# One PSUM bank for a scanned chunk, and a new order around it, in a hybrid decoder layer

## The chip, the cores and the metric

The kernel runs on one core of a Trainium2 chip. Its time is device time in microseconds (us) of one execution. TensorE (PE in the rows) multiplies, and its results go to PSUM, which holds eight banks of 128 partitions x 512 float32. VectorE (DVE) and ScalarE (ACT) read those banks; GpSimd (POOL) does small work and issues some transfers; SP issues the others. Each engine works through its own list of instructions in the order in which the program wrote them, and waits where an instruction needs something that is not there yet.

## The reference

One layer over 512 tokens of width 1024, all in float32:

```
u = rmsnorm(x); proj = u @ w_in            # retention q,k,v,gate; DeltaNet q,k,v,z,beta,a; two merge gates
ro = retention_chunkwise(rotary(rq), rotary(rk), rv)         # 8 heads, chunks of 128
y_ret = (silu(rgate) * groupnorm(ro)) @ w_ret_br
qkv = silu(causal_dwconv(dq, dk, dv))                        # 8 heads of 128
do = gated_delta_chunkwise(l2norm(q), l2norm(k), v, g, beta) # 4 chunks of 128 per head, in turn
    # per chunk: v_new = u_n - w_n S ; o = q_n S + a_n v_new ; S = S d_n + k_n^T v_new
y_dn = (rmsnorm(do) * silu(dz)) @ w_dn_br
h = x + (sigmoid(gate_r)*y_ret + sigmoid(gate_d)*y_dn) @ w_o
h = h + conv_ffn(rmsnorm(h)); out = rmsnorm(h)
```

## The kernel before

Dense products are split into a high and a low part (`whi`, `wlo`), three matmuls for each block of 128 rows; such three are called a triple here. The names in the rows tell the stage: `pk`, `pq`, `pv` are the projections of a DeltaNet head's k, q and v, `pr` those of retention, `pz` the gates, `py` the branch and merge products. Then follow the output product (`po`) and the FFN (`pa`, `pb`, `pd`).

The DeltaNet heads come in two groups of four. `k_front`, `q_front` and `v_front` take a head's projections: a convolution of three DVE instructions on the PSUM bank, a silu on ACT, transposes on TensorE (`pkt`, `pqt`, `pvt`), norms, and for k the products `pkk`, from which DVE makes `A`. A head's decay tile `gb` is loaded from DRAM by `decay_tile` and passed twice through ACT (`Abs`, then `Exp`); `A` and the masked scores need it. `solve` and `solve_up` (`pm`) invert the triangular systems of a group, and then `scan` runs twice, for two pairs of heads side by side: for each of four chunks it multiplies the state by k (`psc<-Sn,k`), lets DVE make `R`, multiplies by the inverse (`psc<-R,tt`), lets ACT copy the result to `vn`, makes the state's update and the chunk's output from `vn`, and lets DVE make the next state `Sn`. `scan_end` normalises, and its transposes are `pot`.

Retention has four pairs of heads. `ret_back` starts one pair after the other: `ret_scores` (`prs`, `pkv`), `ret_state` (`rS`, a chain of DVE and ACT), `ret_out` (`pro`, 28 row entries of the trace on two banks), and `ret_norm`, in which DVE reads both `pro` banks twice before they are free (`st`, then `ro`); its transposes are `proT`.

All PSUM tiles come from one pool of eight banks (`PS(name)`). A new tile takes a free one, and its first product waits until the last reader of the tile that held the bank before is done. The order of work is not written by hand. While the program is being built, a planner (`Order`) keeps a clock that each product advances by an assumed time (`Products.turn` and `Products.matmul`), and an assumed end for each DVE, ACT and POOL instruction. Side tasks (generators) are put between the dense products when that clock reaches their time. So the numbers of the planner set only the order in the lists. The lists themselves are fixed when the kernel runs.

Of the kernel before, what the change touches and what calls it, by code (L numbers as in the profile page):

```python
# [13 lines left out]
AF = mybir.ActivationFunctionType  # L14
ALU = mybir.AluOpType
# [4 lines left out]
P = 128  # L20
T = 512
D = 1024
NT = T // P
# [181 lines left out]
class Products:  # L205
# [3 lines left out]
    part = other = False  # L209

    def turn(self, part, other):


        if part != self.part:
            self.order.product(0.1)
        if self.other and not other:
            self.order.product(0.08)
        self.part, self.other = part, other

    def matmul(self, out, lhsT, rhs, start, stop, **kw):  # L220
        m = max(lhsT.shape[-1], out.shape[-1])
        if lhsT.dtype == F32R:
            self.turn(False, False)
            self.order.product(0.0135 + max(256, out.shape[-1]) / 2400)
        else:
            self.turn(min(lhsT.shape[0], lhsT.shape[-1]) < P, True)
            self.order.product(0.0107 + max(2 * m, 4 * out.shape[-1], 64) / 2400)
        self.engine.matmul(out, lhsT, rhs, start=start, stop=stop, **kw)  # L228

    def transpose(self, out, in_, identity):  # L230
# [5 lines left out]
def body(nc, tc, ctx, io):  # L236
# [3 lines left out]
    vec = Engine(order, "vec", nc.vector, vec_cost)  # L240
    act = Engine(order, "act", nc.scalar, act_cost)
    pool = Engine(order, "pool", nc.gpsimd, pool_cost)
    pe = Products(order, nc.tensor)
# [22 lines left out]
    def PS(name):  # L266
        return psp.tile([P, T], F32, name=name, tag="ps")

    def v3(ap, n=4):
        return ap.rearrange("p (n f) -> p n f", n=n)  # L270
# [384 lines left out]
    beta, G, nG, eG, egl, ekd = (hn(n) for n in ("beta", "G", "nG", "eG", "egl", "ekd"))  # L655
# [76 lines left out]
    def decay_tiles(hs):  # L732
        while "G" not in have:
            yield 0.3
        for h in hs:
            while h == GH and "up" not in heads[GH - 1]["got"] or h > GH and "o" not in heads[h - GH - 1]["got"]:
                yield 0.3
            spawn(decay_tile(h))
            yield 9.0 if h < GH else 4.0
# [11 lines left out]
    def conv_silu(ps, ci, name):  # L751
        w = prm[:, P_CW + 4 * ci:P_CW + 4 * ci + 4]
        acc = S(name)
        act.activation(acc, ps, AF.Identity, scale=w[:, 3:4])
        yield
        for j in (2, 1, 0):
            s = 3 - j
            vec.scalar_tensor_tensor(acc[:, s:], ps[:, :T - s], w[:, j:j + 1], acc[:, s:], ALU.mult, ALU.add)
        yield
        act.activation(acc, acc, AF.Silu)  # L760
        yield
        return acc

    GH = 4
# [20 lines left out]
    def k_front(hd, ps):  # L785
        h = hd["h"]
        kT = hd["kT"] = yield from conv_silu(ps, 8 + h, f"k{h}")
        yield PW
        pkt = transpose4(kT, "pkt")
        pkk = PS("pkk")  # L790
        for n in range(NT):
            pe.matmul(pkk[:, ck(n)], kT[:, ck(n)], kT[:, ck(n)], start=True, stop=True)
        yield -0.8
        A = hd["A"] = S(f"A{h}")
        ktok = hd["ktok"] = S(f"ktok{h}")
        ssk = s4("ssk")
        for n in range(NT):
            act.activation(A[:, ck(n)], pkt[:, ck(n)], AF.Square, accum_out=ssk[:, n:n + 1])
        while "G" not in have:
            yield 0.3  # L800
        for n in range(NT):
            act.activation(ktok[:, ck(n)], pkt[:, ck(n)], AF.Identity, scale=ekd[:, h, n:n + 1])
        yield -0.9
        vec.tensor_scalar(ssk, ssk, EPS, None, ALU.add)
        rk = s4("rk")
        yield
        rsqrt(rk, ssk)
        yield
        while h not in em:
            yield 0.3  # L810
        c1, c2, s = (mini.tile([P, 4], F32, name=n, tag=n, bufs=10) for n in ("c1", "c2", "sr"))
        vec.tensor_tensor(c1, beta[:, h], rk, ALU.mult)
        vec.tensor_tensor(s, c1, rk, ALU.mult)
        vec.scalar_tensor_tensor(c2, s, -1.0, eG[:, h], ALU.mult, ALU.mult)
        for n in range(NT):
            vec.scalar_tensor_tensor(A[:, ck(n)], pkk[:, ck(n)], s[:, n:n + 1], em[h][:, ck(n)], ALU.mult, ALU.mult)
        yield
        pool.affine_select(v3(em[h]), v3(em[h]), [[0, NT], [1, P]], ALU.is_ge, 0.0, base=0, channel_multiplier=-1)
        hd["c1"], hd["c2"] = c1, c2
        yield  # L820
        for b in range(4):
            sp.dma_start(a_dram[h // GH][b, h % GH].rearrange("n i j -> i n j"), v3(A)[R32[b], :, R32[b]])
        hd["got"].add("k")
# [130 lines left out]
    def scan(pair, i):  # L954

        while not all({"q", "v"} <= hd["got"] for hd in pair):
            yield 0.3
        E = range(len(pair))

        o = [hd["vtok"] for hd in pair]  # L960
        ssqo = [s4("ssqo") for _ in E]
        st = [None for _ in E]
        for n in range(NT):
            c = ck(n)
            ps = [v3(PS("psc")) for _ in E]
            R = [hd["vtok"][:, c] for hd in pair]
            if n > 0:
                for e in E:
                    pe.matmul(ps[e][:, 0], pair[e]["kT"][:, c], st[e], start=True, stop=True)
                yield  # L970
                R = [small.tile([P, P], F32, name="R", tag="R", bufs=4) for _ in E]
                for e, hd in enumerate(pair):
                    vec.scalar_tensor_tensor(R[e], ps[e][:, 0], hd["c2"][:, n:n + 1], hd["vtok"][:, c], ALU.mult, ALU.add)
                yield
            for e in E:
                pe.matmul(ps[e][:, 1], tt_all[:, (i + e) * NT + n], R[e], start=True, stop=True)
            yield
            vn = [small.tile([P, P], F32, name="vn", tag="vn", bufs=4) for _ in E]
            for e in E:
                act.copy(vn[e], ps[e][:, 1])  # L980
            yield
            for e, hd in enumerate(pair):
                if n < NT - 1:
                    pe.matmul(ps[e][:, 3], hd["ktok"][:, c], vn[e], start=True, stop=True)
                if n > 0:
                    pe.matmul(ps[e][:, 2], hd["qT"][:, c], st[e], start=True, stop=False)
                pe.matmul(ps[e][:, 2], hd["attn"][:, c], vn[e], start=(n == 0), stop=True)
            yield
            if n < NT - 1:
                for e, hd in enumerate(pair):  # L990
                    sn = small.tile([P, P], F32, name="Sn", tag="Sn", bufs=8)
                    if n == 0:
                        vec.tensor_copy(sn, ps[e][:, 3])
                    else:
                        vec.scalar_tensor_tensor(sn, st[e], egl[:, hd["h"], n:n + 1], ps[e][:, 3], ALU.mult, ALU.add)
                    st[e] = sn
                yield
            for e, hd in enumerate(pair):
                act.activation(o[e][:, c], ps[e][:, 2], AF.Identity, scale=hd["rqs"][:, n:n + 1])
                spawn(scan_ssq(o[e][:, c], ssqo[e][:, n:n + 1]), 0.4)  # L1000
            yield
        for e, hd in enumerate(pair):
            spawn(scan_end(hd, o[e], ssqo[e]), 0.8 + 0.8 * e)
# [75 lines left out]
    def ret_scores(hp):  # L1079

        pss = [PS("prs") for _ in range(2)]
        for n in range(NT):
            for r, ps in zip(E64, pss):
                pe.matmul(ps[:, ck(n)], rkT[n][r, hp], rqT[n][r, hp], start=True, stop=True)
        pk = PS("pkv")
        for n in range(NT - 1):
            for e, r in enumerate(E64):
                vv = rv[n][hp // 2][:, ck(2 * hp % 4 + e)]
                pe.matmul(pk[r, ck(n)], krot[n][:, hp, r], vv, start=True, stop=True)
        yield  # L1090
        states[hp] = [None]
        sTs = [S("sT") for _ in range(2)]
        for sT, ps in zip(sTs, pss):
            vec.tensor_tensor(v3(sT), v3(ps), umask.unsqueeze(1).to_broadcast([P, NT, P]), ALU.mult)
        return sTs, pk
# [58 lines left out]
    def ret_back():  # L1154
        while any(a is None for a in (*rqT, *rkT, *(b for a in rv for b in a))):
            yield 0.3
        for hp in range(4):
            while "up" not in heads[GH - 1]["got"]:
                yield 0.3
            sTs, pk = yield from ret_scores(hp)  # L1160
            yield from ret_state(hp, pk)
            spawn(ret_out(hp, sTs))
            yield 8.0
# [528 lines left out]
```

## Time and profile before

| | |
|---|---|
| three runs | 1001.25 us median (1001.21 to 1002.59) |
| the profiled execution | 1003.4 us, its span 1001.7 us |
| TensorE busy | 979.1 us, 98% of the span |
| VectorE / ScalarE / GpSimd busy | 72% / 53% / 17% |
| mean granted TensorE clock | 0.992 |

TensorE is busy in nearly every slice of the span. Its granted clock is a share of 2.4 GHz: 1.00 is that level, 0.50 is 1.2 GHz, and a stretch with a value between holds some of both. A busy engine at the lower level still counts as busy.

### The profile page before, as it was taken

Reading aid. Unit: us, or ns where it says so; the run is one execution under the profiler, and the core shown is the slowest. Engines: PE = TensorE matmul, PEld = TensorE weight load, DVE = VectorE, ACT = ScalarE, POOL = GpSimd, SP = SyncE. Lnnn points to the kernel's source line nnn. Section 1 sums busy time; section 2 is a strip of 40 time slices with the busy share of each in tenths; the row PEclk is TensorE's granted clock in tenths of the full one; section 3 lists DMA queues with packets and bytes.
Section 4 is the critical chain, followed back from the end, with each engine's and each line's share of the span. In section 5 each row is a group of like instructions: output and inputs, shape, how many; then the busy total and the mean of one; then the engine's idle time right before and its main releaser. Section 6 shows DMA issues by size and latency. Waiting matters only on the chain.

```text
span 1001.7 us, 14270 instructions
## 1 busy us (share of the span) xinstructions
PE 979.1 (98%) x5241; PEld 823.1 (82%) x5241; DVE 725.0 (72%) x1328; ACT 534.0 (53%) x1118; POOL 169.2 (17%) x214
## 2 busy tenths in 40 slices
PE   8999999998999999999999999899999999999997
PEld 7888888877888888888888878798888888888886
DVE  5777798565586797557699989965555667678785
ACT  5599312254865432476677565764443433356663
POOL 3021213222342310032000000121122221000001
PEclk9999999999899999999999999999999999999999
DMA  7243669886497694359986764566669999346663
GB/s 265 71 155 102 186 198 251 239 164 155 145 221 220 210 215 127 127 133 260 279 233 202 275 192 134 169 232 219 214 197 198 225 205 207 103 125 200 190 197 118
DMA packets 82230, 189.29 MB, mean 189 GB/s; under 512 B 22704, under 2 KB 31216, under 8 KB 82160
## 3 DMA queue, kind: packets, MB, share of 16 engines
q1 hardware_dynamic: 54640, 123.36, 38.1%
q0 software_dynamic: 27520, 65.02, 29.4%
q8 instruction: 41, 0.67, 0.3%
q14 instruction: 29, 0.24, 0.1%
HBM read 185.17 MB, written 68.19 MB: 253 GB/s over the span
## 4 chain that ended last, share of the span: by engine, by line
PE 88%; DVE 4%; ACT 3%; DMA 2%; issue 1%; POOL 1%; SPq 0%; POOLq 0%; ACTq 0%; DVEq 0%
PE py L228 14%; PE pb L228 12%; PE pa L228 12%; PE pd L228 10%; PE pr L228 9%; PE pz L228 9%; PE pv L228 4%; PE pq L228 4%; PE pk L228 4%; PE psc L228 3%; PE po L228 1%; PE pm L228 1%; DVE wlo L200 1%; PE pro L228 1%; DMA wraw<-s 1%
## 5 line engine op out<-in xcount | busy, mean ns | idle before, releaser
L200 ACT CAST whi<-wraw 128x1024 fp32r<-128x1024 f32 x212 | 219.3, 1035 | 157.2 <-PE pr L228 66.3
L200 DVE TENSOR_TENSOR wlo<-wraw,whi 128x1024 fp32r<-128x1024 f32 x212 | 254.8, 1203 | 62.5 <-ACT whi L200 59.3
L200 POOL TENSOR_SCALAR tock<-tick 128x1 f32<-128x1 f32 x72 | 33.7, 469 | 399.0 <-ACT tick L200 398.9
L200 DVE SCALAR_TENSOR_TENSOR acc<-pb,prm,acc 128x511 f32<-128x511 f32 (+1 forms) x44 | 33.0, 750 | 57.0 <-ACT acc L200 56.2
L228 PE MATMUL pa<-u2lo,whi 128*128 128x512 f32 (+1 forms) x192 | 71.4, 372 | 0.0
L228 PE MATMUL pa<-u2hi,whi 128*128 128x512 f32 (+1 forms) x192 | 71.4, 372 | 0.0
L228 PE MATMUL pa<-u2hi,wlo 128*128 128x512 f32 (+1 forms) x192 | 71.3, 371 | 0.0
L228 PE MATMUL pb<-u2hi,whi 128*128 128x512 f32 (+1 forms) x184 | 70.0, 380 | 0.0
L228 PE MATMUL pb<-u2lo,whi 128*128 128x512 f32 (+1 forms) x184 | 69.9, 380 | 0.0
L228 PE MATMUL pb<-u2hi,wlo 128*128 128x512 f32 (+1 forms) x184 | 69.9, 380 | 0.0
L228 PE MATMUL py<-whi,oh 128*128 128x512 f32 x160 | 62.7, 392 | 0.0
L228 PE MATMUL py<-wlo,oh 128*128 128x512 f32 x160 | 62.3, 390 | 0.0
L228 PE MATMUL py<-whi,ol 128*128 128x512 f32 x160 | 62.3, 389 | 0.0
L228 PE MATMUL pd<-whi,T 128*128 128x512 f32 (+1 forms) x198 | 55.3, 366 | 0.0
L228 PE MATMUL pz<-uhi,whi 128*128 128x512 f32 x128 | 51.8, 405 | 0.0
L228 PE MATMUL pr<-whi,uhi 128*128 128x512 f32 x128 | 51.2, 400 | 0.0
L228 PE MATMUL pr<-whi,ulo 128*128 128x512 f32 x128 | 50.0, 390 | 0.0
L228 PE MATMUL pz<-uhi,wlo 128*128 128x512 f32 x128 | 49.9, 390 | 0.0
L228 PE MATMUL pz<-ulo,whi 128*128 128x512 f32 x128 | 49.9, 390 | 0.0
L228 PE MATMUL pr<-wlo,uhi 128*128 128x512 f32 x128 | 49.9, 390 | 0.0
L200 DVE SCALAR_TENSOR_TENSOR acc<-pa,prm,acc 128x511 f32<-128x511 f32 (+1 forms) x44 | 33.0, 749 | 19.0 <-ACT acc L200 18.2
L200 ACT ACTIVATE acc<-pb,prm 128x512 f32<-128x512 f32 x22 | 17.2, 780 | 48.5 <-PE pb L228 48.5
(319 smaller groups left out, 2451.9 us busy)
## 6 DMA issues: line engine op xcount, KB each, us to landing
wraw<-w SPq DMA_DIRECT2D x100, 512.0 KB, 4.8
s<-wm POOLq DMA_DIRECT2D x30, 1024.0 KB, 8.8
wraw<-s SPq DMA_DIRECT2D x60, 512.0 KB, 3.9
s<-wd POOLq DMA_DIRECT2D x24, 704.0 KB, 5.5
wraw<-wm SPq DMA_DIRECT2D x30, 512.0 KB, 4.4
s<-s POOLq DMA_DIRECT2D x10, 1024.0 KB, 12.1
wraw<-wd SPq DMA_DIRECT2D x15, 512.0 KB, 3.7
s<-s POOLq DMA_DIRECT2D x8, 704.0 KB, 9.2
```

The source lines that it names most:

```text
L200: return f(out, *args, **kw)
L228: self.engine.matmul(out, lhsT, rhs, start=start, stop=stop, **kw)
```

## The change

It has four parts. In `scan`, a pair's chunk takes one PSUM bank in place of two: head e uses two quarters of it, `qa` for the product with the state and then for the output, `qb` for the product with the inverse and then for the state's update. In `ret_back`, a retention pair waits in the planner until both heads of the pair before are normalised, and 1.5 us more. In `decay_tiles` and `k_front`, a head of the second group (h >= 4) waits in the planner until head h-4 has left its scan (`"o"`): its decay tile, and now also its `pkt` and `pkk`. Last, the planner's clock for products on a part of the array is other: a turn costs 0.2 in place of 0.1, and such a product half of what it did, unless it is 64x64.

```diff
         if part != self.part:
-            self.order.product(0.1)
+            self.order.product(0.2)
...
-            self.turn(min(lhsT.shape[0], lhsT.shape[-1]) < P, True)
-            self.order.product(0.0107 + max(2 * m, 4 * out.shape[-1], 64) / 2400)
+            part = min(lhsT.shape[0], lhsT.shape[-1]) < P
+            self.turn(part, True)
+
+            two = part and tuple(lhsT.shape) != (64, 64)
+            self.order.product((0.0107 + max(2 * m, 4 * out.shape[-1], 64) / 2400) / (1 + two))
...
-            while h == GH and "up" not in heads[GH - 1]["got"] or h > GH and "o" not in heads[h - GH - 1]["got"]:
+            while h >= GH and "o" not in heads[h - GH]["got"]:
                 yield 0.3
             spawn(decay_tile(h))
...
         kT = hd["kT"] = yield from conv_silu(ps, 8 + h, f"k{h}")
+
+        while h >= GH and "o" not in heads[h - GH]["got"]:
+            yield 0.3
         yield PW
         pkt = transpose4(kT, "pkt")
...
-            ps = [v3(PS("psc")) for _ in E]
+
+
+            ps = v3(PS("psc"))
+            qa, qb = [ps[:, 2 * e] for e in E], [ps[:, 2 * e + 1] for e in E]
...
-                    pe.matmul(ps[e][:, 0], pair[e]["kT"][:, c], st[e], start=True, stop=True)
+                    pe.matmul(qa[e], pair[e]["kT"][:, c], st[e], start=True, stop=True)
...
-                pe.matmul(ps[e][:, 1], tt_all[:, (i + e) * NT + n], R[e], start=True, stop=True)
+                pe.matmul(qb[e], tt_all[:, (i + e) * NT + n], R[e], start=True, stop=True)
...
-                    pe.matmul(ps[e][:, 3], hd["ktok"][:, c], vn[e], start=True, stop=True)
+                    pe.matmul(qb[e], hd["ktok"][:, c], vn[e], start=True, stop=True)
                 if n > 0:
-                    pe.matmul(ps[e][:, 2], hd["qT"][:, c], st[e], start=True, stop=False)
-                pe.matmul(ps[e][:, 2], hd["attn"][:, c], vn[e], start=(n == 0), stop=True)
+                    pe.matmul(qa[e], hd["qT"][:, c], st[e], start=True, stop=False)
+                pe.matmul(qa[e], hd["attn"][:, c], vn[e], start=(n == 0), stop=True)
...
         for hp in range(4):
-            while "up" not in heads[GH - 1]["got"]:
+
+            while "up" not in heads[GH - 1]["got"] or len(normed) < 2 * hp:
                 yield 0.3
+            yield 1.5
             sTs, pk = yield from ret_scores(hp)
```

What this does to the lists is seen at three places. The first is TensorE's list at the second retention pair, during the first group's scans. Before, with the tiles' numbers:

```order
L228 MATMUL prs_2360<-rqT0_1465,rkT0_1674 128x128
L228 MATMUL prs_2361<-rqT0_1465,rkT0_1674 128x128
...
L228 MATMUL pkv_2370<-rv20_1845,krot2_1638 64x128 x2
L228 MATMUL psc_2395<-Sn_2325,k0_529 128x128
L228 MATMUL psc_2396<-Sn_2327,k1_643 128x128
L233 MATMUL proT_2403<-cst_101,ro_2351 128x128 x4
L228 MATMUL pq_2337<-uhi1_155,whi_1933 128x512
```

And now, from the same retention pair on:

```order
L236 MATMUL proT_2412<-cst_101,ro_2357 128x128 x4
L231 MATMUL prs_2417<-rqT0_1465,rkT0_1674 128x128
L231 MATMUL prs_2418<-rqT0_1465,rkT0_1674 128x128
...
L231 MATMUL pkv_2427<-rv20_1845,krot2_1638 64x128 x2
L231 MATMUL pq_2349<-uhi4_158,whi_1933 128x512
...
L231 MATMUL psc_2387<-R_2402,tt_178 128x128
L231 MATMUL psc_2387<-R_2403,tt_178 128x128
L236 MATMUL proT_2457<-cst_101,ro_2382 128x128 x4
L231 MATMUL psc_2468<-Sn_2435,k0_529 128x128
L231 MATMUL psc_2468<-Sn_2437,k1_643 128x128
```

The pair's scores now stand behind the first transposes of the pair before, dense triples follow them, and a chunk of two heads has one tile (`psc_2468`) where it had two (`psc_2395`, `psc_2396`). In the program as built, `psc_2396` took the bank of the second `pro` tile before it.

The second place is TensorE's list at the end of those scans, up to the k projection of head 5. Before (the third retention pair, in the middle of four chunks):

```order
L228 MATMUL pv_2624<-uhi2_156,whi_2007 128x512
...
L228 MATMUL prs_2649<-rqT0_1465,rkT0_1674 128x128
L228 MATMUL prs_2650<-rqT0_1465,rkT0_1674 128x128
...
L228 MATMUL pkv_2659<-rv01_2057,krot0_1605 64x128 x2
...
L228 MATMUL psc_2569<-R_2609,tt_178 128x128
L228 MATMUL psc_2570<-R_2610,tt_178 128x128
L228 MATMUL psc_2579<-R_2616,tt_178 128x128
L228 MATMUL psc_2580<-R_2617,tt_178 128x128
```

And now (the third pair comes when the scans are over, and `pkt`, `pkk` of head 4 come after it):

```order
L236 MATMUL proT_2666<-cst_101,ro_2627 128x128 x4
L231 MATMUL prs_2673<-rqT0_1465,rkT0_1674 128x128
...
L236 MATMUL pkt_2695<-cst_101,k4_2353 128x128 x4
L231 MATMUL pkk_2700<-k4_2353 128x128 x4
L236 MATMUL proT_2706<-cst_101,ro_2644 128x128 x4
L236 MATMUL pot_2721<-cst_101,vtok0_867 128x128 x4
L236 MATMUL pot_2731<-cst_101,vtok1_1002 128x128 x4
L231 MATMUL pv_2515<-uhi7_161,whi_2007 128x512
...
L231 MATMUL pk_2785<-uhi0_154,whi_2109 128x512
```

Head 4's k front has moved from the middle of the scans (behind `pq` of head 4) to their end, and the last product here, `pk_2785`, takes the bank of `pkt_2695`.

The third place is ScalarE's list there, now:

```order
L200 ACTIVATE roT2_2719<-proT_2666,prm_103 128x512
L200 ACTIVATE gb4_2671<-gb4_2671,nG_172 128x128 x4
L200 ACT_TABLE_LOAD
L200 ACTIVATE gb4_2671<-gb4_2671 128x512
L200 ACTIVATE A4_2751,ssk_2753<-pkt_2695 128x128 x4
L200 ACTIVATE ktok4_2752<-pkt_2695,ekd_175 128x128 x4
L200 ACTIVATE rS_2744<-rS_2744,cst2_102 128x128
L200 ACTIVATE roT3_2765<-proT_2706,prm_103 128x512
L200 ACTIVATE doT0_2767<-pot_2721,prm_103 128x512
...
L200 ACTIVATE gb6_2798<-gb6_2798,nG_172 128x128 x4
```

Before, the first tile of the four (`gb4`) stood far ahead, between the first chunk's copies:

```order
L200 COPY vn_2183<-psc_2148 128x128
L200 ACTIVATE gb4_2152<-gb4_2152,nG_172 128x128 x4
L200 ACT_TABLE_LOAD
L200 ACTIVATE gb4_2152<-gb4_2152 128x512
L200 COPY vn_2201<-psc_2178 128x128
```

The work on `gb4` has moved behind the scans, ahead of the two readers of `pkt_2695`, and on SP's list the loads of `gb6` and `gb7` now stand behind the four small transfers of head 4's `A`.

## Rows read from the trace of the kernel before

**Rows 1.** The page's head and its TensorE line.

```profile
span 1001.7 us, 14270 instructions
...
PE 979.1 (98%) x5241; PEld 823.1 (82%) x5241; DVE 725.0 (72%) x1328; ACT 534.0 (53%) x1118; POOL 169.2 (17%) x214
```

**Rows 2.** Stages: length, PE, PEld, DVE, ACT, POOL busy, PEclk, DMA share, GB/s.

```profile
220.00:225.00 5.00, 2.51 (x23) 1.83 (x23) 4.96 (x12) 1.74 (x2) 1.05 (x1) 0.99 0.67 106
225.00:230.00 5.00, 5.00 (x25) 4.18 (x24) 0.67 (x3) 3.38 (x17) 0.00 (x0) 0.67 0.86 212
...
245.00:250.00 5.00, 1.99 (x20) 1.64 (x22) 4.96 (x12) 0.63 (x1) 1.20 (x1) 0.88 0.64 76
250.00:255.00 5.00, 5.00 (x30) 4.67 (x27) 1.05 (x3) 2.00 (x12) 0.00 (x0) 0.50 1.08 270
255.00:260.00 5.00, 5.00 (x35) 4.61 (x35) 1.70 (x9) 4.66 (x19) 2.46 (x4) 0.94 0.37 129
```

**Rows 3.** All waits of TensorE from 195 to 285 us: total, times, longest.

```profile
PE psc L228 <- DVE ro L200: 1.9, 1, 1.9
PE prs L228 <- DVE q L200: 1.6, 1, 1.6
PE pkv L228 <- DVE ro L200: 1.3, 1, 1.3
PE pvt L233 <- ACT v L200: 1.0, 1, 1.0
PE prs L228 <- DVE ro L200: 0.7, 1, 0.7
PE psc L228 <- ACT ktok L200: 0.7, 1, 0.7
PE proT L233 <- DVE sT L200: 0.6, 1, 0.6
```

**Rows 4.** The chain that ended last, in order of time: start, us, what.

```profile
202.21 0.44 PE psc L228 x4
202.66 1.09 PE prs L228 x16
203.75 0.81 PE pkv L228 x12
...
208.82 1.38 PE pk L228 x6
...
211.09 3.10 PE pro L228 x28
...
221.97 1.27 DVE ro L200 x4
...
228.52 1.15 ACT A L200 x8
229.66 1.04 ACT ktok L200 x4
...
261.88 0.45 PE pot L233 x4
...
263.04 1.16 ACT gb L200 x4
264.22 1.28 ACT L200
265.52 0.63 ACT gb L200
```

**Rows 5.** TensorE in order of time, dense products after a scan product, and head 5's.

```profile
205.84 0.48 PE L228 MATMUL pk<-uhi,whi 128*128 128x512 f32 x1
206.16 0.39 PE L228 MATMUL pk<-ulo,whi 128*128 128x512 f32 x1
...
266.58 0.48 PE L228 MATMUL pk<-uhi,whi 128*128 128x512 f32 x1
```

**Rows 6.** Transfers of the decay tiles, 190 to 300 us.

```profile
DMA to landing us min/median/max: 3.1/8.2/9.9
```

More of the change, by code (lines that the diff above doesn't have):

```diff
@@ L972, in scan @@
                 for e, hd in enumerate(pair):
-                    vec.scalar_tensor_tensor(R[e], ps[e][:, 0], hd["c2"][:, n:n + 1], hd["vtok"][:, c], ALU.mult, ALU.add)
+                    vec.scalar_tensor_tensor(R[e], qa[e], hd["c2"][:, n:n + 1], hd["vtok"][:, c], ALU.mult, ALU.add)
                 yield
             for e in E:
-                pe.matmul(ps[e][:, 1], tt_all[:, (i + e) * NT + n], R[e], start=True, stop=True)
+                pe.matmul(qb[e], tt_all[:, (i + e) * NT + n], R[e], start=True, stop=True)
             yield
@@ L979, in scan @@
             for e in E:
-                act.copy(vn[e], ps[e][:, 1])
+                act.copy(vn[e], qb[e])
             yield
@@ L992, in scan @@
                     if n == 0:
-                        vec.tensor_copy(sn, ps[e][:, 3])
+                        vec.tensor_copy(sn, qb[e])
                     else:
-                        vec.scalar_tensor_tensor(sn, st[e], egl[:, hd["h"], n:n + 1], ps[e][:, 3], ALU.mult, ALU.add)
+                        vec.scalar_tensor_tensor(sn, st[e], egl[:, hd["h"], n:n + 1], qb[e], ALU.mult, ALU.add)
                     st[e] = sn
@@ L998, in scan @@
             for e, hd in enumerate(pair):
-                act.activation(o[e][:, c], ps[e][:, 2], AF.Identity, scale=hd["rqs"][:, n:n + 1])
+                act.activation(o[e][:, c], qa[e], AF.Identity, scale=hd["rqs"][:, n:n + 1])
                 spawn(scan_ssq(o[e][:, c], ssqo[e][:, n:n + 1]), 0.4)
```

## The prediction

> **What bounds the kernel now.** I read the page first: TensorE is busy 979.1 of 1001.7 us [rows 1]. So a reordering can win only what TensorE does not do at full speed: about 22 us of idle time, and the time in which it is busy at a lower clock, which the busy sum hides. The stages show where both lie. Nearly all of what this change touches is between 220 and 260 us, in the first group's scans: in 220 to 225 and in 245 to 250 TensorE is busy 2.51 and 1.99 of 5 us while VectorE is busy 4.96 of 5, and behind each of the two the granted clock is low, 0.67 in 225 to 230 and 0.50 (1.2 GHz) in 250 to 255 [rows 2]. The table of waits names the reason [rows 3]: in six waits, together 6.8 us, TensorE stands in front of a bank that a reader has not left: four on VectorE's `ro`, `q` and `sT` for the next retention pair, one on `ro` for a scan's product (1.9 us), one on ScalarE's `ktok`. The seventh, 1.0 us at about 274 us, waits for data (head 4's v behind the decay tiles on ScalarE). The chain of waits shows the same from the other side: VectorE's second `ro` runs from 221.97 to 223.24 [rows 4], as its list puts k's convolution and a weight's low part ahead of it, and TensorE's next product needs the bank that it reads.
>
> **How much is there.** I count the work of TensorE's list from the first scan product (202.21 us [rows 4]) to the first product of head 5's k (266.58 us [rows 5]), 64.4 us. Prices: a dense product 0.23 (1.38 for six), a scan product 0.22 (0.44 for two; the rows count each twice), a pair's scores 1.09 + 0.81, its outputs 3.10, four transposes 0.45 [rows 4], and 0.09 more for the first dense product after other work (0.32 between the two starts in place of 0.23 [rows 4, 5]). In the list: 63 dense (14.5), 68 scan products (15.0), three scores (5.7), three outputs (9.3), ten groups of transposes (4.5), `pkk` and `pqk` with eight products (1.8), nine returns to dense (0.8): 51.6 us. So 12.8 us of the 64.4 are lost. The six waits are 6.8 of them. The clock is another 4.7: (1 - 0.67) x 5 = 1.65, 0.50 x 5 = 2.5, 0.06 x 5 = 0.3, 0.05 in 220 to 225, and of the 0.6 in 245 to 250, in which TensorE mostly stood, some 0.2 [rows 2]. 1.3 us stay unnamed (hand-overs of a tenth or two each); I let them stay.
>
> **Part by part.** The *planner's clock* and its turns are numbers at build time; they cost nothing on the chip, and act only through the order. *One bank for a pair's chunk* takes four tiles out of each round of the two scans down to two, so that of eight banks two more are free for `prs`, `pkv`, `pro`. *Pairs in turn* moves each pair's `prs`/`pkv` behind the `proT` of the pair before, and so behind both of its `ro`. *Head 4's front held back* takes `pkt`/`pkk`, four `A` instructions and ScalarE's A and `ktok` (1.15 + 1.04 [rows 4]) out of the scans and puts them behind, with the tile's two passes and its table load (1.16 + 1.28 + 0.63 = 3.1 us [rows 4]), which stood at 202 us before.
>
> I then went through the changed lists of the three engines by hand from 202.2 us, each instruction at its duration before, and looked at each place where TensorE takes a bank or data:
> - The first retention pair ends on TensorE at about 216. VectorE's second `ro` still comes behind k's convolution and the weight's low part, and ends at about 225.8. The bank goes to `psc_2468`, which by the count of products ahead of it is issued at 228.7. The 1.9 us wait is gone, with 3 us to spare.
> - `psc_2387`'s R, then `Sn`, `vn`: VectorE and ScalarE are done 0.7 to 1.6 us ahead of TensorE each time, since three or four triples lie where none did.
> - The third pair's scores are issued at 244.2; their banks were left at 236 to 238. `pkk_2700` comes at 246.6, and the `ro` whose bank it takes ends at 242.9.
>
> So all six old waits have cover, and with them goes the cause of the low clock: 6.8 + 4.7 = 11.5 us. What hides the bank's readers is the dense triples of pq and pv that now stand between the scan's steps; without them the old waits come back. The 1.0 us wait for head 4's v also goes (ScalarE has its silu ready some 1.5 us ahead by the same count): 12.5.
>
> What is late next: by work alone TensorE comes to `pk_2785` at 202.2 + 47.3 = 249.5 (two outputs in place of three, nine groups of transposes, no `pqk`, eleven returns). It takes the bank of `pkt_2695`. ScalarE reads the last scan outputs until 245.4, `roT` until 246.0, then `gb4` 3.1, A 1.15, `ktok` 1.04: 251.3. A new wait of 1.3 to 1.8 us; I take 1.5. It is shorter than the pairs of waits that stood ahead of a low clock before, so I take no clock loss with it. Queued behind `ktok` on ScalarE are `roT3` and `doT0` to `doT3`, whose banks TensorE wants next; they follow within 2 us and TensorE has five triples by then. One more of the kind: head 5's q goes through ScalarE late, its transposes wait some 1.2 us at 271. The list has six more returns to dense over both groups: 6 x 0.09 = 0.5. In the second group I found no wait that the change touches; the scan is now spread over more gate triples and into the first `py`, so nothing is gained or lost there. The second solve keeps its place in TensorE's list within two triples.
>
> Sum: 12.5 - 1.5 - 1.2 - 0.5 = 9.3 us. The profiled execution took 1003.4 (span 1001.7 [rows 1] and 1.7 around it), 2.15 above the median of 1001.25; taken off the median the sum gives **992.0 us**, off the profiled one 994.1.
>
> **What the shared bank costs.** In the rows before, head 0's `Sn` may start when head 0's three products are done, as head 1's go to another bank. With one bank it starts after all six: 3 x 0.22 = 0.66 us later, and the steps at `R` and `vn` each wait for the second head's product, 0.22 each: 1.1 us for a chunk on the scan's own chain [rows 4]. I take it at nothing, since other triples cover it. The Trainium skill, "PSUM — Partial Sum Buffer", section "PSUM bank collisions raise a hardware error", asks for exactly this: two engines are to be kept apart by bank, not by address, even where one head's columns are not the other's. By that rule the sharing is not free; no run here shows it yet. If no triple covered it, three chunks of two groups would give 2 x 3 x 1.1 = 6.6 us.
>
> **The rivals.** *A, the forecast*: 992, range 989 to 994.5. The lower end is 12.5 with neither new wait at full size.
> *B, ScalarE becomes the late engine at `pk_2785`*: `gb4`'s load is issued behind a weight's load, by my count at 237; loads of these tiles took 3.1, 8.2 at the middle and 9.9 us at most [rows 6]. At 9.9 it lands at 247 and `ktok` at 252.3; a later issue adds as much. With some 3 us of wait there and the clock low for 4 to 5 us after it (2 to 2.5 more), the time is 992 + 4 = 996. For it: ScalarE's list has no gap there. Against it: at 8.2 the tile is there first.
> *C, the shared bank's chain shows*: 992 + 6.6 = 998.6, or the old waits return at other banks. Against it: the margins above are 0.7 us and more at nearly every step.
> *D, slower*: `gb6` and `gb7` stand on SP behind head 4's `A`, which stands behind `gb4`. If each load takes 9.9 us or more and `gb4` is late besides, `gb6` lands after 266, and ScalarE, which works in order, keeps head 4's v, the third pair's last state and head 5's k behind it. TensorE needs the state at about 269 and would get it at 274.5, then run at the low clock: 5.6 + 3, and again for head 5. From about 4 us above the longest load seen this eats all of the 9.3 us; then the time is 1002 to 1006.
>
> **How the numbers follow.** A 0.66, B 0.18 (994.5 to 998.5), C 0.10 (998.5 to 1002), D 0.06. Two tenths of a per cent, 2 us, is about what a measurement of this kernel can tell from no change. Faster by more (below 999.25): A, B and a third of C, 0.87. Within: 0.08. Slower: 0.05. The range that holds eight in ten takes A and B: 989 to 998; A's own is 989 to 994.5.
>
> **What would show it.** Right: between 220 and 260 us no wait of TensorE on `ro`, `q` or `sT` above 0.3 us, granted clock 0.95 and more in each stage of 5 us there, and the first product of head 5's k at 251 to 253 in place of 266.58. The one wait there is on `ktok`. The second group as before. Wrong: a wait on `gb` in ScalarE's rows, or on `R`, `vn` or `Sn` in TensorE's; a stage below 0.8 in the clock; or a new wait of TensorE after 300 us, where I looked for none.

## The result, and the profile after

The changed kernel takes 991.0 us (median of 4 runs, 989.93 to 992.75), the kernel before beside it 1001.67 (4 runs, 1001.21 to 1002.59): a ratio of 0.9894, 95% interval 0.9876 to 0.9912. The forecast was 992.0. The profiled execution of the changed kernel took 991.78 us, its span 989.7.

The page's head and TensorE line of the changed kernel (before: [rows 1]):

```profile
span 989.7 us, 14268 instructions
...
PE 971.2 (98%) x5241; PEld 816.3 (82%) x5241; DVE 723.5 (73%) x1328; ACT 530.1 (54%) x1116; POOL 165.8 (17%) x214
```

The share of busy time reads 98% in both and tells nothing. The stages do (the columns of [rows 2]); the same five as there, of the changed kernel:

```profile
220.00:225.00 5.00, 5.00 (x44) 4.54 (x44) 4.93 (x10) 3.45 (x12) 1.62 (x3) 1.00 0.02 6
225.00:230.00 5.00, 5.00 (x46) 4.31 (x43) 4.09 (x13) 2.92 (x12) 0.06 (x1) 1.00 1.08 211
...
245.00:250.00 5.00, 4.80 (x45) 4.21 (x43) 3.02 (x7) 4.97 (x17) 2.45 (x4) 1.00 0.89 130
250.00:255.00 5.00, 4.26 (x21) 3.51 (x22) 1.73 (x8) 4.97 (x13) 1.64 (x2) 1.00 0.50 89
255.00:260.00 5.00, 5.00 (x28) 4.29 (x27) 4.18 (x6) 4.50 (x12) 0.00 (x0) 1.00 0.41 125
```

VectorE is still busy 4.93 of the 5 us from 220 on; what is gone is TensorE standing behind it, and with it the clocks of 0.67 and 0.50. The whole list of TensorE's waits from 195 to 285 us, seven before [rows 3], is now one row:

```profile
PE pk L231 <- ACT ktok L200: 0.9, 1, 0.9
```

It is the wait at `pk_2785`. The chain of waits of the changed kernel leads to it (start, us, what), and the next fence has it in TensorE's own order:

```profile
202.57 0.44 PE psc L231 x4
...
244.93 0.57 ACT roT L200
245.50 1.17 ACT gb L200 x4
...
247.98 0.63 ACT gb L200
248.62 1.03 ACT A L200 x8
249.65 1.05 ACT ktok L200 x4
```

```profile
250.74 0.50 PE L231 MATMUL pk<-uhi,whi 128*128 128x512 f32 x1 [0.94 <-ACT ktok L200]
```

Head 5's first product starts at 250.74; before, at 266.58 [rows 5]. From the first scan product (202.57; 202.21 before [rows 4]) that is 48.2 us in place of 64.4.

How much of the whole this is, in stages of 100 us, first of the kernel before, then of the changed one:

```profile
0.00:100.00 100.00, 95.91 (x554) 83.35 (x555) 68.99 (x154) 76.57 (x186) 19.40 (x28) 0.98 0.45 148
200.00:300.00 100.00, 92.25 (x648) 79.65 (x647) 64.09 (x205) 60.79 (x192) 34.92 (x42) 0.95 0.74 172
```

```profile
0.00:100.00 100.00, 93.48 (x552) 80.85 (x553) 68.69 (x153) 75.90 (x186) 19.26 (x27) 1.00 0.44 148
200.00:300.00 100.00, 99.06 (x715) 86.02 (x714) 72.25 (x221) 65.19 (x208) 37.62 (x46) 1.00 0.81 199
```

In 200 to 300 us TensorE's idle time falls from 7.75 to 0.94 (6.8 us), and the clock from a loss of 0.05 x 92.25 = 4.6 to none: 11.4 us of the 11.6 between the two profiled executions. In the first 100 us, which the change does not mean to touch, the changed run stood 2.4 us longer and lost 1.9 us less to the clock. That part is not the change's: `u1_two_banks` below, with the changed kernel's own lists, stood 6.7 us there and had a clock of 0.98, as the kernel before had; the changed kernel itself stood 6.5 us at 1.00.

### The profile page after: what moved, and what is told of

Same layout as the page of the kernel before. It is cut to its first block, busy times and chain, and to the rows that moved or that the text cites. A ratio compares the mean times of both kernels' runs of the same rounds, so it can differ in the third digit from the quotient of the medians.

```text
span 989.7 us, 14268 instructions
## 1 busy us (share of the span) xinstructions
PE 971.2 (98%) x5241; PEld 816.3 (82%) x5241; DVE 723.5 (73%) x1328; ACT 530.1 (54%) x1116; POOL 165.8 (17%) x214
## 4 chain that ended last, share of the span: by engine, by line
PE 89%; DVE 3%; DMA 2%; ACT 2%; issue 1%; POOL 1%; SPq 0%; POOLq 0%; DVEq 0%; ACTq 0%
PE py L231 13%; PE pb L231 12%; PE pa L231 12%; PE pd L231 10%; PE pr L231 9%; PE pz L231 9%; PE pv L231 4%; PE pq L231 4%; PE pk L231 4%; PE psc L231 3%; PE po L231 2%; PE pm L231 1%; PE pro L231 1%; DVE wlo L200 1%; DMA wraw<-s 1%
## 5 line engine op out<-in xcount | busy, mean ns | idle before, releaser
L200 POOL TENSOR_SCALAR tock<-tick 128x1 f32<-128x1 f32 x72 | 30.3, 421 | 401.4 <-ACT tick L200 401.4
```

Of the source, the lines that this page charges most:

```text
L200: return f(out, *args, **kw)
```

## Experiments

Theory: the time went to TensorE standing at banks whose readers were late, and to the low clock behind some of these stands; any order or supply of banks that puts enough products in between takes it away. Rivals: the two banks set free do it all (1), the shared bank has a cost of its own that is hidden in the 991 (2), moving head 4's front does it (3), the planner's other times do it (4). Every run stands beside runs of the kernel before.

| run | parts of the change in it | median us (range) | ratio to before, 95% |
|---|---|---|---|
| changed kernel | all four | 991.0 (989.9 to 992.8) | 0.9894 (0.9876 to 0.9912) |
| `u1_two_banks` | all but the bank | 991.8 (990.5 to 992.9) | 0.9897 (0.9883 to 0.9912) |
| `u2_pairs_free` | all but pairs in turn | 990.5 (989.2 to 991.2) | 0.9881 (0.9865 to 0.9896) |
| `u3_front_early` | all but the front held | 991.2 (990.4 to 993.8) | 0.9898 (0.9883 to 0.9913) |
| `u4_old_clock` | all but the planner's times | 994.3 (993.8 to 994.6) | 0.9922 (0.9909 to 0.9936) |
| `a1_one_bank` | the bank alone | 992.8 (992.7 to 994.0) | 0.9911 (0.9894 to 0.9927) |
| `a2_in_turn` | pairs in turn alone | 1002.2 (1000.2 to 1004.0) | 1.000 (0.999 to 1.001) |
| `a3_front_held` | the front held alone | 998.4 (996.5 to 999.0) | 0.996 (0.9944 to 0.9975) |
| `a4_new_clock` | the planner's times alone | 1003.4 (1001.3 to 1005.5) | 1.0014 (1.0005 to 1.0024) |
| `c14_bank_and_clock` | the bank and the times | 995.5 (994.2 to 996.7) | 0.9935 (0.992 to 0.995) |
| `a2_gb6_early` | in turn, one load earlier | 992.2 (991.1 to 993.9) | 0.9904 (0.9889 to 0.9919) |
| `d3_ro_late` | all, VectorE 3.8 us later once | 993.8 (993.0 to 994.9) | 0.9922 (0.9905 to 0.9938) |
| `d6_ro_late` | all, VectorE 7.6 us later once | 999.0 (998.1 to 1002.7) | 0.9977 (0.9966 to 0.9989) |

### One part undone

**Two banks again**, on the changed kernel:

```diff
-            ps = v3(PS("psc"))
-            qa, qb = [ps[:, 2 * e] for e in E], [ps[:, 2 * e + 1] for e in E]
+            ps = [v3(PS("psc")) for _ in E]
...
```

Expected: 

> The changed kernel with one part undone: a pair's chunk takes two banks again. The lists of the three engines stay as they are in the scans; only the banks differ. Counted with the times of the changed kernel's trace: the second retention pair's scores then take the bank of the transposes just ahead, which ScalarE reads into roT, 0.6 to 0.8 us too late, and its pkv takes the bank that VectorE's second ro reads until 225.9, 0.5 us too late; at the other places the readers are done before. Theory (the time was lost to waits at banks, and to the clock behind them): 1.3 us of waits, too little for a low clock, 991 + 1.3 = about 992.3, not above 994. Rival 1 (it is the two banks set free that win the time): the waits of before come back, 6 us and more, 997 to 1000. Rival 2 (the shared bank has a cost of its own on the scan's chain, hidden in the 991): 990 or less.

Measured 991.8. All five engines' lists of work are those of the changed kernel, row for row; only the tiles' banks, and with them what waits for what, differ. TensorE's waits from 195 to 285 us:

```profile
PE pk L231 <- ACT ktok L200: 0.7, 1, 0.7
PE prs L231 <- ACT roT L200: 0.4, 1, 0.4
```

The 0.4 us on `roT` is where the count put one; the wait on `ro` beside it did not come. Rivals 1 and 2 fall for this list: with the other three parts in place the freed banks are not needed, and giving them up neither costs nor wins what the runs can tell. What sharing does on the scan's own chain is seen at the second chunk's update (VectorE's `Sn`, and the product it follows). The changed kernel, then two banks:

```profile
211.28 0.38 PE L231 MATMUL psc<-vn,ktok 128*128 128x128 f32 x2
...
212.82 0.61 DVE L200 SCALAR_TENSOR_TENSOR Sn<-Sn,egl,psc 128x128 f32<-128x128 f32 x2 [1.42 <-PE psc L231]
```

```profile
212.87 0.38 PE L231 MATMUL psc<-vn,ktok 128*128 128x128 f32 x2
...
213.80 0.35 DVE L200 SCALAR_TENSOR_TENSOR Sn<-Sn,egl,psc 128x128 f32<-128x128 f32 x1 [1.03 <-issue]
214.47 0.35 DVE L200 SCALAR_TENSOR_TENSOR Sn<-Sn,egl,psc 128x128 f32<-128x128 f32 x1 [0.32 <-PE psc L231]
```

With two banks the first head's `Sn` starts 0.93 us after its product, with one bank 1.54: 0.61 later (0.66 was forecast). In the same chunk the copy to `vn` starts 0.64 us after its product in place of 0.42, the 0.22 that was forecast. The Trainium skill, "PSUM — Partial Sum Buffer", section "PSUM bank collisions raise a hardware error", has engines kept apart by bank, not by address. The trace shows a program that keeps to it, as the first head's `Sn` waits for the second head's products too; no run here shows what would happen without that wait. Its price is covered here.

**Pairs not in turn, front early, old planner times**, each alone undone on the changed kernel:

```diff
-            while "up" not in heads[GH - 1]["got"] or len(normed) < 2 * hp:
+            while "up" not in heads[GH - 1]["got"]:
                 yield 0.3
-            yield 1.5
```

Expected: 

> The changed kernel with one part undone: retention pairs follow one another without waiting for the norm of the pair before. TensorE then comes to the second proT some 7.3 us after the first pair's pro, while VectorE's second ro ends 9.6 us after it, behind st, k's convolution and a weight's low part. Theory: a wait of 2 to 2.5 us on ro there, another of about 1 us behind it on R, and 1 to 2 us of a lower clock: 995 to 997. Rival 1 (the banks set free win it all): no wait above 0.5 us, 991 to 992. Rival 3 (head 4's front held back wins it): 991 to 993, as that part still stands.

```diff
-            while h >= GH and "o" not in heads[h - GH]["got"]:
+            while h == GH and "up" not in heads[GH - 1]["got"] or h > GH and "o" not in heads[h - GH - 1]["got"]:
                 yield 0.3
...
-        while h >= GH and "o" not in heads[h - GH]["got"]:
-            yield 0.3
         yield PW
```

Expected: 

> The changed kernel with one part undone: decay tiles and k fronts of the second group as early as before. By the places of pkv and pkt behind the first pair's pro (8.2 and 10.9 us, against 5 and 9.6 us for the two ro) no bank is waited for, and ScalarE's A and ktok have their tile early, so that the 0.9 us wait on ktok goes too. Theory: 990 to 992, no slower than the changed kernel; this part of the change then brings nothing in these lists. Rival 3 (the front in the middle of the scans is what made VectorE late): A's four instructions, 1.1 us, and the rest push the next ro and R back, 2 to 4 us of waits with a lower clock behind them, 994 to 997.

```diff
-            self.order.product(0.2)
+            self.order.product(0.1)
...
-            self.order.product((0.0107 + max(2 * m, 4 * out.shape[-1], 64) / 2400) / (1 + two))
+            self.order.product(0.0107 + max(2 * m, 4 * out.shape[-1], 64) / 2400)
```

Expected: 

> The changed kernel with one part undone: the planner's old times for products on a part of the array. It moves triples against side work over the whole program. Theory: the first pair's pro and the second pair's scores stay 7.5 us and its transposes 9.4 to 10.3 us apart, so the second ro (9.6) is nearly covered; small waits of 1 to 3 us in all and little of the clock, 992 to 995. Rival 4 (the other clock, by better distances everywhere, is what wins): 998 or more, with waits on ro, R or sT above 1 us each and a low clock in the first group's scans.

`u3_front_early` (991.2) and `u4_old_clock` (994.3) came out in the expected range, the second with 4.2 us of waits in 195 to 285 where 1 to 3 were expected; those are 3.3 more than the changed kernel's 0.9, and the medians differ by 3.3. `u2_pairs_free` did not: 990.5, and one wait of 0.4 us. The count had taken VectorE's list from the changed kernel. The planner had put both `ro` ahead of k's convolution here, and the second is done (219.8) before its transposes. VectorE's second `ro`, TensorE's transposes of it, and k's convolution:

```profile
218.48 1.36 DVE L200 TENSOR_SCALAR ro<-pro,mv,rgn 128x128 f32<-128x128 f32 x4
...
221.56 0.60 PE L236 MATMUL proT<-cst,ro 128*128 128x128 f32 x4
...
222.61 2.32 DVE L200 SCALAR_TENSOR_TENSOR k<-pk,prm,k 128x511 f32<-128x511 f32 x3 [0.24 <-ACT k L200]
```

So no part but the planner's times is missed when it is taken away. That does not say that the parts do nothing; for that they must stand alone.

### One part alone

The same edits, each by itself on the kernel before. **The bank:**

```diff
-            ps = [v3(PS("psc")) for _ in E]
+            ps = v3(PS("psc"))
+            qa, qb = [ps[:, 2 * e] for e in E], [ps[:, 2 * e + 1] for e in E]
...
```

Expected: 

> The kernel before with one part alone: one bank for a pair's chunk. The list of products hardly moves; the banks do. From the first pair's pro TensorE has 6.7 us of work to the product that takes the bank of the first ro, and 9 us to pkt, which takes that of the second ro; VectorE needs some 7 to 8 and 9.6 us. Theory (what counts is how many microseconds of products stand between a pro and the next tile that takes its bank, whichever part puts them there): waits on ro of 1 to 2 us in place of 3.9, pkv and prs of the third pair free, about half of the 10.7 us won: 994 to 997. Rival 1 (the two banks set free are the gain): 991 to 993. Rival 2 (this part brings nothing): 1000 to 1002.

Measured 992.8, lower than expected. TensorE's waits in 195 to 295 us:

```profile
PE proT L233 <- DVE ro L200: 1.2, 1, 1.2
PE pvt L233 <- ACT v L200: 1.0, 1, 1.0
PE pkv L228 <- DVE q L200: 0.5, 1, 0.5
PE pkk L228 <- DVE sT L200: 0.4, 1, 0.4
PE pkt L233 <- DVE ro L200: 0.2, 1, 0.2
```

This run changes one thing: all five engines' lists of work are those of the kernel before, row for row, and only the tiles' banks, and the waits that go with them, differ. The six bank waits of 6.8 us [rows 3] came down to 2.3. At the second retention pair, where they were 1.9 on `ro` and 0.6 on `sT`, 0.2 and 0.4 are left: the bank that VectorE's second `ro` reads is not wanted until `pkt`, four transposes and two triples later than before. In 200 to 300 us TensorE stands 3.2 us in place of 7.75, at a clock of 1.00 in place of 0.95:

```profile
200.00:300.00 100.00, 96.79 (x695) 83.20 (x693) 67.98 (x211) 66.53 (x210) 37.02 (x45) 1.00 0.82 199
```

That is 4.5 + 4.6 = 9.1 us, and the medians differ by 9.1 (1001.9 of the kernel before, run beside it). So the freed banks are a cause by themselves, and rival 1 is right for the old list.

**Pairs in turn:**

```diff
-            while "up" not in heads[GH - 1]["got"]:
+            while "up" not in heads[GH - 1]["got"] or len(normed) < 2 * hp:
                 yield 0.3
+            yield 1.5
```

Expected: 

> The kernel before with one part alone: retention pairs in turn. From the first pair's pro TensorE now has 9.6 us of work before the products that take the banks of the two ro. Theory: waits of up to 1 us there, one of 0.7 to 1 us on ktok of head 4 (A and ktok stand 2.3 us ahead of the product that takes their bank), no low clock: 993 to 995. Rival 1 (two banks set free are needed): waits of 4 us and more, a low clock, 997 to 1001.

Measured 1002.2: no gain, the largest miss. The old waits on banks are down to 2.0 us, but a new one of 7.7 us eats it, at a bank whose reader stands behind a load. In order of time, SP's, ScalarE's and TensorE's rows of it, and then what SP waited for before:

```profile
246.99 0.35 SPq L298 DMA_DIRECT2D wraw<-w  x1
247.44 1.17 SPq L743 DMA_DIRECT2D gb<-g_dram  x2
...
256.07 1.28 ACT L200 ACTIVATE gb<-gb,nG 128x128 f32<-128x128 f32 x4 [8.53 <-DMA gb<-g_dram]
...
259.69 0.79 PE L228 MATMUL pk<-uhi,whi 128*128 128x512 f32 x1 [7.68 <-ACT vtok L200]
```

```profile
SPq L298 <- DVE wlo L200: 11.5, 1, 11.5
```

The load of head 6's tile stands on SP behind a weight's load, which waits 11.5 us for VectorE's `wlo`. It is issued at 247.4 us, so ScalarE, which works in order, stands with the last scan outputs behind it, and TensorE waits for their bank. The clock is low after it:

```profile
255.00:260.00 5.00, 0.31 (x1) 0.31 (x2) 0.00 (x0) 3.90 (x11) 0.53 (x2) 0.73 0.21 77
260.00:265.00 5.00, 5.00 (x14) 3.90 (x14) 3.05 (x8) 4.97 (x18) 3.75 (x4) 0.58 0.63 210
```

**The front held, and the planner's times:**

```diff
-            while h == GH and "up" not in heads[GH - 1]["got"] or h > GH and "o" not in heads[h - GH - 1]["got"]:
+            while h >= GH and "o" not in heads[h - GH]["got"]:
                 yield 0.3
...
+        while h >= GH and "o" not in heads[h - GH]["got"]:
+            yield 0.3
         yield PW
```

Expected: 

> The kernel before with one part alone: decay tiles and k front of the second group held back. From the first pair's pro TensorE has 6.5 us of work to the product on the first ro's bank and 7.4 us to that on the second's, which VectorE ends at 9.6. Theory: one wait of 2 to 3 us, with 1 to 2 us of a lower clock behind it, the later ones gone in part: 996 to 999. Rival 3 (the front in the middle of the scans was the cause): 991 to 993.

```diff
-            self.order.product(0.1)
+            self.order.product(0.2)
...
+            two = part and tuple(lhsT.shape) != (64, 64)
+            self.order.product((0.0107 + max(2 * m, 4 * out.shape[-1], 64) / 2400) / (1 + two))
```

Expected: 

> The kernel before with one part alone: the planner's other times for products on a part of the array. From the first pair's pro TensorE has 6.3 us to pkv, on the first ro's bank, and 7.5 us to a scan product on the second's. Theory: waits on ro of 2 us and more there, on the third pair's scores too, a low clock behind at least one: 997 to 1001. Rival 4 (the clock of the planner is the gain): 991 to 994.

The front alone gave 998.4, in the range, but by another wait than foreseen (luck, then): 5.2 us on `ro`, whose cause is two engines away. GpSimd's rows, then TensorE's:

```profile
263.85 0.21 POOL L200 TENSOR_SCALAR tock<-tick 128x1 f32<-128x1 f32 x1 [7.08 <-ACT tick L200]
...
264.93 2.04 POOL L200 TENSOR_TENSOR rgn<-rvar,mhalf 128x4 f32<-128x4 f32 x2
...
266.49 1.44 PE L233 MATMUL proT<-cst,ro 128*128 128x128 f32 x4 [5.20 <-DVE ro L200]
```

GpSimd stands for a mark (`tick`) that ScalarE sets behind its passes over the decay tiles, and the norm's `rgn` stands behind that. The planner's times alone gave 1003.4, above the expected range and no faster than before: waits on `ktok` (2.3), `ro` (1.9) and `q` (1.8), and a clock of 0.54 in 245 to 250.

### Tests of the mechanism

**The load moved**, on pairs in turn alone:

```diff
-        gb = S(f"gb{h}")
-        sp.dma_start(gb, row_of(g_dram, h))
+        for j in (5, 6) if h == 5 else [h] if h != 6 else ():
+            gbs[j] = S(f"gb{j}")
+            sp.dma_start(gbs[j], row_of(g_dram, j))
+        gb = gbs[h]
```

Expected: 

> The kernel with pairs in turn alone (1002.2), and one transfer moved: the load of decay tile gb6 is issued right behind that of gb5, ahead of a weight's load that stands 11.5 us on SP for VectorE's wlo; the lists of TensorE, VectorE, ScalarE and GpSimd stay as they are. Theory: in the run with pairs in turn ScalarE stood 8.5 us for gb6's load, TensorE 7.7 us behind it, and the clock was 0.73 and 0.58 in the two stages after (2.2 us). With the load there in time all of it goes: 1002.2 - 7.7 - 2.2 = 992.3, range 991.5 to 994.5. Rival 7 (the load is only the last of several things that are late there): a wait of 3 us or more on vtok stays, 995 to 1000.

Measured 992.2. TensorE's waits are now

```profile
PE pkv L228 <- DVE ro L200: 1.0, 1, 1.0
PE psc L228 <- ACT ktok L200: 0.6, 1, 0.6
PE psc L228 <- ACT roT L200: 0.4, 1, 0.4
```

One transfer, one place further ahead on SP, is worth 10 us here: the wait of 7.7 and the clock behind it. Rival 7 of that run falls, and pairs in turn, too, can bring nearly the whole gain without the bank.

**VectorE made late at one place**, on the changed kernel (k = 3, then 6; the lists are otherwise as they are):

```diff
         ro = S("ro")
+        for n in range(k * NT if h == 1 else 0):
+            n %= NT
+            nc.vector.tensor_scalar(ro[:, ck(n)], po[:, ck(n)], mv[:, n, 0:1], rr[:, n:n + 1], ALU.subtract, ALU.mult)
         for n in range(NT):
```

With k = 3. Expected: 

> The changed kernel, with VectorE made later at one place and every list otherwise as it is: the four instructions of the first pair's second ro are issued three times over ahead of themselves, unknown to the planner (same values written again), 3.8 us. In the changed kernel the R behind that ro ends at 226.4 and its product starts at 227.7, so TensorE has 1.3 us of cover there and 2.3 at the transposes. Theory (waits beyond the cover count, and the low clock only behind a long stand): one wait of about 2.5 us on R, later readers covered; the clock may fall by up to 1.7 us after it, as it did behind the 2.5 us idle of before: 993.5 to 995.5. Rival 1 (the cover is deep, the banks alone matter): 991 to 992. Rival 5 (all of VectorE's delay goes through): 994.8 and a clock loss on top.

With k = 6. Expected: 

> As the run with ro three times over, but six times: 7.6 us more on VectorE at the one place. Theory: a wait of about 6.3 us on R and 2.5 us or more of lost clock behind it: 991 + 6.3 + 2.5 = 999.8, range 998.5 to 1001.5. Rival 6 (the clock behind a stand is not a cost, as the engine has slack afterwards): 997.3.

The one new wait of TensorE, and the stages around it, first with the 3.8 us:

```profile
229.79 0.71 PE L231 MATMUL psc<-R,tt 128*128 128x128 f32 x4 [2.42 <-DVE R L200]
```

```profile
227.00:230.00 3.00, 0.58 (x3) 0.21 (x2) 3.00 (x11) 0.00 (x0) 0.00 (x0) 1.00 1.09 266
230.00:232.00 2.00, 2.00 (x15) 1.61 (x14) 2.00 (x6) 1.68 (x9) 0.00 (x0) 1.00 1.08 271
```

And with the 7.6 us, VectorE's row of what was added ahead:

```profile
226.22 7.74 DVE L1155 TENSOR_SCALAR ro<-pro,mv,rgn 128x128 f32<-128x128 f32 x24
...
235.82 1.23 PE L231 MATMUL psc<-R,tt 128*128 128x128 f32 x4 [6.25 <-DVE R L200]
```

```profile
235.00:240.00 5.00, 4.18 (x17) 3.90 (x18) 3.48 (x11) 3.02 (x12) 0.86 (x2) 0.52 0.00 0
```

The waits came within 0.1 us of the count (2.5 and 6.3). The first costs 993.8 - 991.0 = 2.8 us with the clock at 1.00; the second 8.0 us, beside 6.25 of waiting and 0.48 x 4.18 = 2.0 of lost clock. So the cover at this place is some 1.5 us (7.74 - 6.25; 1.3 by the count), a stand beyond it counts in full, and the clock behind a long stand counts on top (rivals 1, 5 and 6 of these runs fall).

**The bank and the planner's times** (both diffs above, on the kernel before). Expected: 

> The kernel before with two parts: one bank for a pair's chunk, and the planner's other times. Theory (distance between a pro and the next tile or transposes that need its ro): with the other times the list brings the second pair's transposes 7.1 and 7.5 us behind the first pro in place of 9, and pkv of the third pair 4 us behind the second pro on the bank of its first ro, so the waits of 2 to 3 us come back: 994 to 998, slower than one bank alone (992.8). Rival 1 (with the banks free the order matters little): 990 to 992.

Measured 995.5, in the range and slower than the bank alone, but mainly by another wait than was named, so the number was in part luck. The transposes find their `ro` done, and the first scan product behind them waits 1.94 us for VectorE's `A` in the bank of `pkk`. VectorE had itself stood 2.73 us for GpSimd's `rk`, which, as with the front held, comes behind a `tick` of ScalarE. The second wait is on `ro` at `pkv`, as named, but of 0.8 us. Rival 1 falls in this list: with the banks free the order still costs 2.7 us against the bank alone.

## Why the prediction was right

- **The six bank waits and the clock behind them (11.5 us).** All six are gone, and the clock is 1.00 in each stage. The stretch that was counted fits: 47.3 us of work were forecast from the first scan product to `pk_2785`; 250.74 - 0.94 - 202.57 = 47.2 were measured. So do the places: the second `ro` was to end at 225.8 and ended at 225.9, the third pair's scores were to start at 244.2 and did at 243.9.
- **The wait for head 4's v (1.0 us).** Gone.
- **The new wait at `pk_2785`.** There, on `ktok`, as named; 0.94 us in place of 1.5, as ScalarE reached the tile's passes half a microsecond earlier than counted (245.50, not 246.0).
- **The 1.2 us at head 5's q.** Did not come. These two terms were too large by 0.6 and 1.2; with them right the sum is 11.1 in place of 9.3, beside 10.7 between the medians. The 0.5 us for more returns to dense products is in both sums; no run measures it by itself. Off 1001.25, 11.1 would have given 990.2, about as far below the 991.0 as 992.0 lies above: the near hit is in part luck and does not measure how well these two terms were sized.
- **The shared bank.** Its price on the scan's chain is real and was sized rightly (0.61 for the first head's `Sn`, 0.66 forecast; 0.22 at `vn`, 0.22 forecast); that other triples cover it was right.
- **Rivals B and D.** Wrong for this list: the four tiles' loads landed 3.3, 5.1 (middle) and 7.6 us after issue, and ScalarE stood 0.5 us for one, at 258 us. That was named as a sign of being wrong, but here it was short and no wait of TensorE followed from it. Head 5's first product, named for 251 to 253, came at 250.74, and after 300 us TensorE has the same waits as before, each within 0.2 us. But the rivals' mechanism is no invention: with pairs in turn alone it takes the whole gain away.
- **What the prediction overstated.** "Without them the old waits come back", it said of the triples between the scan's steps. With the old lists and one bank they are not there, and 2.3 of 6.8 us came back, with none of the clock. It treated the four parts as one chain; the bank on one side and the new lists, which the other three parts make, on the other are substitutes. Old lists and two banks 1001.7, old lists and one bank 992.8, new lists and two banks 991.8, both 991.0: either is nearly or wholly enough, and the gains do not add. The parts that make the new lists are not substitutes each by itself: alone they gave 1002.2, 998.4 and 1003.4.

## What to carry to other kernels

Before crediting a reordering, count for each shared buffer when its last reader is done, on that engine's list, and how much work stands ahead of the next taker on its own list; a stall beyond that cover costs its length, and a long one (5 us and more here) the clock as well. Undo each part and run each part alone: parts that all remove the same stall look useless one way and may look harmful the other, since each also moves something else, such as a small load behind a blocked one on an in-order queue. When a sensible reordering brings nothing, look for the one wait that took the place of the old ones, and for who queued it.

## What was not expected of the hardware

The clock does not follow the length of a stand alone. A stand of 1.94 us (the bank and the planner's times) was followed by 0.57 over four us, of 2.42 us (VectorE 3.8 us late) by 1.00 throughout. The first, and the stage behind it, of the run with the bank and the times:

```profile
226.26 1.13 PE L231 MATMUL psc<-Sn,k 128*128 128x128 f32 x4 [1.94 <-DVE A L200]
```

```profile
226.00:230.00 4.00, 3.74 (x11) 3.13 (x12) 3.12 (x10) 0.80 (x2) 0.64 (x1) 0.57 1.12 197
```

Just ahead of that stand TensorE had done a pair's scores, two scan products and eight transposes; ahead of the other, six dense products. But with the planner's times alone a stand of 2.3 us behind four transposes left the clock at 1.00, so that is not settled as the reason:

```profile
219.83 1.16 PE L231 MATMUL pkk<-k 128*128 128x128 f32 x8 [2.26 <-ACT ktok L200]
```

```profile
220.00:225.00 5.00, 5.00 (x52) 4.30 (x53) 2.38 (x11) 2.49 (x13) 2.65 (x3) 1.00 1.01 173
```

In the same run two stands of 1.86 and 1.83 us close together, at the third pair's scores, came with the clock of 0.54 in 245 to 250. The stands of 5.2, 6.25 and 7.7 us were all followed by a low clock (0.50, 0.52, 0.58). What decides it for the shorter ones stays open.
